# Two-layer decoder trunk on one core: one more pair of rows by seven products in each group of the last stage

## The chip, the cores and the metric

The kernel runs on one core of a Trainium2 chip. Its time is the device time of one execution in microseconds (us). The engines are named as in the profile: PE (TensorE, matmuls; PEld its weight loads), DVE (VectorE), ACT (ScalarE), POOL (GpSimd), SP (SyncE, which issues the loads).

## The reference

Two decoder layers over 256 tokens of width 2048, in float32. Layer 0 mixes tokens by retention, layer 1 by a short convolution; each is followed by a SwiGLU feed-forward network (FFN). Only the last FFN is touched by the change:

```python
D_MODEL, SEQ = 2048, 256
D_FF = 5632

def swiglu(h, w_in, w_out):
    a, b = jnp.split(h @ w_in, 2, axis=-1)
    return (jax.nn.silu(a) * b) @ w_out

h = (rms_norm(x, norm2_g[i]) * (1.0 + sc2) + sh2).astype(x.dtype)
x = (x + g2 * swiglu(h, ffn_w_in[i], ffn_w_out[i])).astype(x.dtype)
...
return rms_norm(x, final_g).astype(x.dtype)
```

## The kernel before

**Precision.** Each weight block and each activation is held as two numbers, `hi` (a cast to the matmul's own float32 form) and `lo` (the rest). A product is three matmuls: hi by hi, hi by lo, lo by hi (`thrice`, L460 to L462). A weight block therefore needs a cast on ACT (L402) and a subtraction on DVE (L405) before PE can use it.

**Loads.** All weights lie in memory in the order of use, in chunks of 128 x 2048 (1 MB). `fetch` issues one chunk on SP into one of three `raw` buffers; it waits until the chunk before in that buffer has been split. `prepare` splits a chunk in pieces; the `hi` and `lo` pieces have four buffers each. `take` hands blocks to PE and prepares up to three pieces (`AHEAD` + 1) beyond the one in use.

**The last stage** is the FFN of layer 1, in two parts of 20 and 24 tiles of 128 hidden columns. The matmuls put tokens on the output's partitions: one covers 128 tokens (of two halves), 128 rows of the weight and 512 of its columns. The last four tiles of part 0 are made first in another form (`first_rows`).

- *First matrix* (`last_input`): ten groups, four in part 0 and six in part 1. A group makes 512 columns of `a` and the matching 512 of `b`, over 16 tiles of rows taken as 8 pairs, 0 to 7. At pair 2 (`TURNS_AT`) of the next group its results are transposed and split for the second matrix (`turned`, L1331 to L1336).
- *Second matrix* (`last_output`): in each part two groups of 1024 output columns, over the part's own rows: 10 pairs in part 0, 12 in part 1. The pairs of part 0 are taken in the order 0, 1, 2, 3, 4, 8, 6, 9, 5, 7. In the last group of part 1 the last three pairs (`TAIL_ROWS`) are the tail: they are taken one column block after the other, and the kernel's end (`added`, `stored`) follows them.

**Pairs in sevens.** A pair of row tiles, two column blocks and two token halves are a 2 x 2 by 2 x 2 product of blocks. Ordinarily it is eight products, 24 matmuls of 128 x 512. A pair of class `Seven` does it with seven products (Winograd's form of Strassen's), 21 matmuls. Which pairs these are is set by `IN_SEVEN` (pairs of each group of the first matrix) and `OUT_SEVEN` (pairs of the second matrix, for part 0 and part 1). For that, three more things are computed:

- *Sums of weights*, in `prepare`: an ordinary chunk is two pieces of 1024 columns (0 and 1). A chunk in sevens is four (2 to 5): a difference of 1024 columns (L391, into the tile `x8` of the page's `x`) and two of 512 (L395, L397) on DVE, and a cast and a `lo` for 1024, 1024, 1024 and 512 columns.
- *Sums of tokens* (`tokens_sums_of`, L1143 to L1146 and two to four splits), once for each pair in sevens: for the first matrix in `made_in_sums` ahead of the ten groups, for the second inside `turned`. They are kept in small tiles (`single_sums`, `tokens_sums`).
- *Sums of products* (`mixed_sums`, L1242 to L1246): after the last seven of a group four banks are combined; in the last group of all they are multiplied by the gate and added (`gated`, L1205, L1206) right there.

PE's order is the order of the program. The instructions of DVE and ACT are put in order by a scheduler.

Of the kernel before, what the change touches and what calls it, by code (L numbers as in the profile page):

```python
# [37 lines left out]
LEAD = 6  # L38
ROOTS_AT, SPREAD_AT = 1, 3
TAIL_ROWS = 6  # L40
IN_SEVEN, OUT_SEVEN, TURNS_AT, BESIDE_CB, BESIDE_SUMS = (3, 4, 6), ((2, 4, 6), (2, 4, 6)), 2, 40, 48
LAST_TILES = 20, 24
STORE_AT, LOAD_AT = 0, 2
LEAD_RET, LEAD_CONV, LEAD_FFN = 6, 4, 2
# [97 lines left out]
class Seven:  # L142
# [6 lines left out]
    n = 2 * DV // P  # L149
# [107 lines left out]
def trunk(ctx: ExitStack, tc: tile.TileContext, x_in, c_in, pos_in, w_mod, cols_in, gain_in, tab_in, w_all, out):  # L257
# [12 lines left out]
    def tmp(tag, shape=(P, S), dtype=F32, pool=work, bufs=None):  # L270
        return pool.tile(list(shape), dtype, tag=tag, name=name(tag), bufs=bufs)
# [90 lines left out]
    in_seven, n = set(), 0  # L362
# [146 lines left out]
    def split(dst, src, at=slice(None)):  # L509

        nc.scalar.copy(dst[:, 0, at], src)
        nc.vector.tensor_tensor(dst[:, 1, at], src, dst[:, 0, at].bitcast(F32), op=ALU.subtract)
# [83 lines left out]
    def scaled_only(layer, norm, j):  # L596

        needed(layer, SC2 if norm else SC1, j)
        a = mod_a[layer][norm][:, j : j + 1]
        high, low = raw_all[:, j, ENDS : ENDS + S], raw_all[:, j, ENDS + S :]  # L600
        nc.scalar.activation(high, x[j], AF.Identity, scale=a)
        nc.vector.scalar_tensor_tensor(low, x[j], a, high.bitcast(F32), op0=ALU.mult, op1=ALU.subtract)
# [50 lines left out]
    def output(groups, act, which, last, after=None, base=None):  # L653

        layer, gate = which[0], mod_g[which[0]][which[1] == GT2]
        first, *groups = groups
        base, acc = first.ks[0] if base is None else base, None
        banks = product(first, act, base, last=False)
        for j, g in enumerate(groups):
            needed(*which, j)  # L660
            col = gate[:, j : j + 1]
            if last and j == KT - 1:
                (pt,) = packed(g, act, base)
                nc.vector.scalar_tensor_tensor(x[j], pt[:, 0, :], col, x[j], op0=ALU.mult, op1=ALU.add)
                acc = [acc, squares(None, x[j], "acc1")]
                if after:
                    after(j)
                return acc
            (pt,) = product(g, act, base, banks=banks[j : j + 1])
            t = tmp("sum", bufs=4)  # L670
            nc.vector.scalar_tensor_tensor(t, pt[:, 1, :], col, x[j], op0=ALU.mult, op1=ALU.add)
            nc.vector.scalar_tensor_tensor(x[j], pt[:, 0, :], col, t, op0=ALU.mult, op1=ALU.add)
            if last:
                acc = squares(acc, x[j])
            if after:
                after(j)


    with ExitStack() as inner:
# [64 lines left out]
        with tc.tile_pool(name="start", bufs=1) as sp:  # L744
# [59 lines left out]
            with tc.manual_schedule(engines={mybir.EngineType.DVE, mybir.EngineType.Activation}):  # L804
# [24 lines left out]
                def square(i):  # L829

                    sq = [rm.tile([P, 2, S], F32, tag=f"mid{2 * i + n}", name=name("sq")) for n in range(2)]
                    for n in range(2):
                        nc.scalar.activation(sq[n], x4[i][:, 2 * n : 2 * n + 2, :], AF.Square)
                    return sq
# [5 lines left out]
                acc = square(0)  # L840
# [197 lines left out]
        def ret_out(part, last):  # L1038
            after = (lambda j: scaled_only(0, 1, j)) if last else None
            acc = output(RET_OUT[part], mid, (0, GT1), last, after, base=0)  # L1040
            assert not asides
            for n in range(len(mid)):
                if ("mid", n) in tag_of:
                    free.append(tag_of.pop(("mid", n)))
            return acc
# [5 lines left out]
        acc = ret_out(1, True)  # L1051
# [16 lines left out]
    for part, groups in enumerate(FFN_IN):  # L1068
# [10 lines left out]
        acc = output(FFN_OUT[part], mid, (0, GT2), part == 1, (lambda j: scaled_only(1, 0, j)) if part else None)  # L1079
# [4 lines left out]
    for i, g in enumerate(CONV_IN):  # L1084
        pending += [sums(g)] if i else normed(acc, 1, 0, g)
        while len(pending) >= 3:
# [3 lines left out]
            b, c, u = pb(tmp("bsum", pool=mpool, bufs=2)), pc(), pu()  # L1090
# [12 lines left out]
    acc = output(CONV_OUT, mid, (1, GT1), True, lambda j: scaled_only(1, 1, j))  # L1103
# [19 lines left out]
    def turn(t, c):  # L1123
# [10 lines left out]
    tokens_sums = [  # L1134
        [v.rearrange("p (i n) -> p i n", i=2)] for v in (in_cb[:, : 6 * P], in_cb[:, 6 * P : 12 * P])
    ] + [[mpool.tile([P, 2, 3 * P], F32R, tag="sums_of_tokens", name="sums_of_tokens")]]
    single_sums = [in_cb[:, n * P : (n + 2) * P].rearrange("p (i n) -> p i n", i=2) for n in (12, 14)]

    def tokens_sums_of(a11, a21, a12, a22, third, others):

        u = tmp("u512", (P, DV), pool=mpool, bufs=3)
        s1, s2, s4, s3 = [u[:, n * P : (n + 1) * P] for n in range(4)]
        nc.vector.tensor_tensor(s3, a11, a21, op=ALU.subtract)  # L1143
        nc.vector.tensor_tensor(s1, a21, a22, op=ALU.add)
        nc.vector.tensor_tensor(s2, s1, a11, op=ALU.subtract)
        nc.vector.tensor_tensor(s4, a12, s2, op=ALU.subtract)  # L1146
        split(third, s3)
        n = 3 * P // len(others)
        for i, dst in enumerate(others):
            split(dst, u[:, i * n : (i + 1) * n])  # L1150

    def parts(both):

        return [both[:, i, t * P : (t + 1) * P] for i in range(2) for t in range(2)]
# [3 lines left out]
    def made_in_sums():  # L1158

        tmp("beside_sums", (P, BESIDE_SUMS), bufs=1)  # L1160
        for tag, n in (("u", 3), ("low", 3), ("sum", 4)):
            single_sums.extend(tmp(tag, (P, 2, P), F32R, bufs=n) for _ in range(n))
        for i in IN_SEVEN:
            both = tmp("u512", (P, 2, S), pool=mpool, bufs=3)
            for n in range(2):
                k = 2 * i + n
                high, low = [h[k].bitcast(F32)[:, v, :] for v in range(2)]
                nc.vector.tensor_tensor(both[:, n, :], high, low, op=ALU.add)
            in_sums[i] = [single_sums.pop() for _ in range(3)]
            tokens_sums_of(*parts(both), h[2 * i][:, :, P:], in_sums[i])  # L1170

    def three(v):
        return [v[0][:, :, n * P : (n + 1) * P] for n in range(3)] if len(v) == 1 else v
# [214 lines left out]
    for part in range(2):  # L1388
        n = LAST_TILES[part] // 2
        mid = mids(LAST_TILES[part]) if part else first_mid  # L1390
        if not part:
            first_rows(mid[-2:])
            made_in_sums()
            ahead_now[0] = AHEAD + 1
        for i, groups in enumerate(LAST_IN[part]):
            due = OUT_SEVEN[part]
            seven = [tokens_sums[due.index(q)] if q in due else None for q in (2 * i, 2 * i + 1)]
            last_input(groups, mid[2 * i : 2 * i + 2], seven)
        act = [mid[k // 2][:, k % 2] for k in range(2 * n)]
        for c, groups in enumerate(LAST_OUT[part]):  # L1400
            last_output(part, 2 * c, groups, act, part * LAST_TILES[0])
# [37 lines left out]
```

## Time and profile before

| | us |
|---|---|
| median of 3 runs | 2595.39 (2594.69 to 2596.74) |
| the profiled execution | 2593.25 |
| its span in the profile | 2591.5 |
| busy of this: PE / PEld / DVE / ACT | 2563.3 / 2236.3 / 2197.4 / 1306.0 |
| one group of the first matrix (1976.7 to 2019.3) | 42.6 |
| a middle group of the second matrix, part 1 (2465.8 to 2530.0) | 64.2 |

The ten groups of the first matrix and the four of the second fill the span from about 1923 us to the end. In rows of the profile a group of instructions is given by line, engine, operation, output and inputs with their shapes, the count, and then busy time and mean duration in ns; behind the second bar stands the engine's idle time before these instructions and what ended it. In a timeline the first column is the start, the second the duration. A row of windows gives each engine's busy time in a stretch of the span, the granted clock of TensorE, and the DMA's share and rate.

### The profile page before, as it was taken

The numbers are of one execution on the slowest core, as the hardware profiler recorded it, in microseconds if no ns is written. First come the engines' busy times: TensorE is split into PE (matmuls) and PEld (weight loads), VectorE is DVE, ScalarE is ACT, GpSimd is POOL, SyncE is SP. The second block draws the span as 40 slices with busy tenths as digits, with TensorE's granted clock in tenths as the row PEclk, the third lists the DMA queues.
The fourth block names the chain that finished last, engine by engine and source line by source line (L and its number), as shares of the span: only waits on it lengthen the run. The fifth ranks groups of instructions, "written<-read, shape, count | busy, mean of one in ns | idle before, by whom it ended". The sixth has DMA issues, their size and how long they took to land.

```text
span 2591.5 us, 36408 instructions
## 1 busy us (share of the span) xinstructions
PE 2563.3 (99%) x14181; PEld 2236.3 (86%) x14181; DVE 2197.4 (85%) x2762; ACT 1306.0 (50%) x1792; POOL 125.9 (5%) x232
## 2 busy tenths in 40 slices
PE   7999999999999999999999999999999999999998
PEld 6898889888889888888888898888998888888887
DVE  7988978787698887777778889988989998999978
ACT  5544543444456545334444454444565554556554
POOL 0000000110000000100001001000000000000001
PEclk9999999999999999999999999999999999999999
DMA  9975768767676888777877768877845565555654
GB/s 398 388 293 209 268 243 306 300 248 277 251 282 246 330 323 307 301 296 298 298 294 283 298 237 313 330 297 277 308 165 210 188 223 205 180 210 187 222 208 147
DMA packets 96688, 689.56 MB, mean 266 GB/s; under 512 B 10737, under 2 KB 12161, under 8 KB 13441
## 3 DMA queue, kind: packets, MB, share of 16 engines
q1 hardware_dynamic: 96514, 687.23, 71.3%
q8 instruction: 111, 1.82, 0.3%
q14 instruction: 63, 0.52, 0.1%
HBM read 685.08 MB, written 2.11 MB: 265 GB/s over the span
## 4 chain that ended last, share of the span: by engine, by line
PE 94%; DVE 3%; DMA 2%; issue 1%; ACT 1%; ACTq 0%; POOLq 0%; POOL 0%; DVEq 0%
PE bank L447 30%; PE bank L450 16%; PE bank L461 12%; PE bank L460 12%; PE bank L462 12%; PE bank L495 2%; PE bank L496 2%; PE bank L494 2%; PE bank L627 1%; PE bank L629 1%; PE bank L628 1%; DVE raw L755 1%; DMA raw<-w_all 1%; DVE lo L405 1%; PE bank L983 1%
## 5 line engine op out<-in xcount | busy, mean ns | idle before, releaser
L402 ACT CAST hi<-raw 128x1024 fp32r<-128x1024 f32 (+1 forms) x954 | 978.9, 1033 | 1015.8 <-PE bank L447 346.4
L405 DVE TENSOR_TENSOR lo<-raw,hi 128x1024 fp32r<-128x1024 f32 (+1 forms) x954 | 1133.9, 1197 | 322.6 <-ACT hi L402 317.3
L447 PE MATMUL bank<-h,hi 128*128 128x512 f32 x2016 | 699.3, 390 | 0.0
L450 PE MATMUL bank<-h,lo 128*128 128x256 f32 x2016 | 568.5, 282 | 0.0
L447 PEld LDWEIGHTS bank<-h,hi 128*128 128x128 f32 x2016 | 378.4, 188 | 79.2
L460 PE MATMUL bank<-hi,h 128*128 128x512 f32 x1032 | 405.0, 392 | 2.2 <-DVE rm L739 2.2
L461 PE MATMUL bank<-lo,h 128*128 128x512 f32 x1032 | 404.3, 392 | 0.0
L462 PE MATMUL bank<-hi,h 128*128 128x512 f32 x1032 | 402.7, 390 | 0.0
L450 PEld LDWEIGHTS bank<-h,lo 128*128 128x128 f32 x2016 | 381.0, 189 | 0.1
L318 DVE SCALAR_TENSOR_TENSOR raw<-raw,cb 128x2048 f32<-128x2048 f32 x160 | 365.5, 2284 | 15.7 <-DMA raw<-w_mod 15.3
L447 PE MATMUL bank<-mid,hi 128*128 128x512 f32 x922 | 319.8, 390 | 0.0
L450 PE MATMUL bank<-mid,lo 128*128 128x256 f32 x922 | 260.1, 282 | 0.4 <-DVE lo L405 0.4
L460 PEld LDWEIGHTS bank<-hi,h 128*128 128x128 f32 x1032 | 194.4, 188 | 40.7 <-DVE rm L739 2.8
L462 PEld LDWEIGHTS bank<-hi,h 128*128 128x128 f32 x1032 | 194.2, 188 | 40.8
L461 PEld LDWEIGHTS bank<-lo,h 128*128 128x128 f32 x1032 | 194.5, 188 | 40.4 <-DVE lo L405 3.3
L447 PEld LDWEIGHTS bank<-mid,hi 128*128 128x128 f32 x922 | 173.1, 188 | 36.2
L450 PEld LDWEIGHTS bank<-mid,lo 128*128 128x128 f32 x922 | 174.2, 189 | 0.7 <-DVE lo L405 0.7
L447 PE MATMUL bank<-rm,hi 128*128 128x512 f32 x496 | 172.5, 390 | 0.0
L496 PE MATMUL bank<-h,lo 128*128 128x256 f32 x512 | 146.4, 286 | 4.6 <-DVE lo L405 4.6
L494 PE MATMUL bank<-h,hi 128*128 128x256 f32 x512 | 146.1, 285 | 3.4 <-ACT h L783 3.4
L495 PE MATMUL bank<-h,hi 128*128 128x256 f32 x512 | 146.1, 285 | 0.7 <-DVE h L784 0.7
L450 PE MATMUL bank<-rm,lo 128*128 128x256 f32 x496 | 139.8, 282 | 0.0
(256 smaller groups left out, 3197.4 us busy)
## 6 DMA issues: line engine op xcount, KB each, us to landing
raw<-w_all SPq DMA_DIRECT2D x456, 1024.0 KB, 4.8
raw<-w_mod SPq DMA_DIRECT2D x192, 1024.0 KB, 5.2
x<-x_in SPq DMA_DIRECT2D x4, 512.0 KB, 5.3
out<-xt SPq DMA_DIRECT2D x4, 512.0 KB, 3.0
decay<-tab_in SPq DMA_DIRECT2D x8, 128.0 KB, 2.4
x<-gate_row SPq DMA_DIRECT2D x2, 512.0 KB, 4.8
last_gain<-gain_in SPq DMA_DIRECT2D x1, 1024.0 KB, 7.2
cols<-cols_in SPq DMA_DIRECT2D x1, 152.0 KB, 8.3
```

Of the source, the lines that this page charges most:

```text
L318: nc.vector.scalar_tensor_tensor(raw, raw, 1.0, cb, op0=ALU.mult, op1=ALU.mult, accum_out=total)
L402: nc.scalar.copy(hi, raw)
L405: nc.vector.tensor_tensor(lo, raw, hi.bitcast(F32), op=ALU.subtract)
L447: nc.tensor.matmul(pt, hi, h, start=fresh and k == g.ks[0], stop=False, skip_group_check=True)
L450: nc.tensor.matmul(pt[:, 1, :], lo, h[:, 0, :], start=False, stop=last and k == g.ks[-1], skip_group_check=True)
L460: nc.tensor.matmul(o, hi, w_hi, start=first, stop=False)
L461: nc.tensor.matmul(o, hi, w_lo, start=False, stop=False)
L462: nc.tensor.matmul(o, lo, w_hi, start=False, stop=last)
L494: nc.tensor.matmul(pt, hi, h[:, 0, :], start=first, stop=False, skip_group_check=True)
L495: nc.tensor.matmul(pt, hi, h[:, 1, :], start=False, stop=False, skip_group_check=True)
L496: nc.tensor.matmul(pt, lo, h[:, 0, :], start=False, stop=last, skip_group_check=True)
L627: nc.tensor.matmul(pt, hi, high, start=k == 0, stop=False, skip_group_check=True)
```

## The change

Pair 5 of every group of the first matrix becomes a pair in sevens, so that pairs 3, 4, 5 and 6 of the eight stand in a row. In the second matrix pair 5 in part 0 and pair 8 in part 1 become pairs in sevens; in the order of use they stand at the places 2, 4, 6 and 8 of ten or twelve. That is 14 pairs in sevens more (56 for 42). The additional sums of tokens get tiles of their own from buffers that are free by then.

```diff
-IN_SEVEN, OUT_SEVEN, TURNS_AT, BESIDE_CB, BESIDE_SUMS = (3, 4, 6), ((2, 4, 6), (2, 4, 6)), 2, 40, 48
+IN_SEVEN, OUT_SEVEN, TURNS_AT, BESIDE_CB, BESIDE_SUMS = (3, 4, 5, 6), ((2, 4, 5, 6), (2, 4, 6, 8)), 2, 40, 48
...
     def made_in_sums():
 
         tmp("beside_sums", (P, BESIDE_SUMS), bufs=1)
-        for tag, n in (("u", 3), ("low", 3), ("sum", 4)):
+        for tag, n in (("acc", 1), ("sq", 2), ("u", 3), ("low", 3), ("sum", 4)):
             single_sums.extend(tmp(tag, (P, 2, P), F32R, bufs=n) for _ in range(n))
         for i in IN_SEVEN:
...
             in_sums[i] = [single_sums.pop() for _ in range(3)]
             tokens_sums_of(*parts(both), h[2 * i][:, :, P:], in_sums[i])
+        tokens_sums.append([single_sums.pop() for _ in range(3)])
```

## The prediction

> **What bounds the kernel now.** I read the page first, then the windows of the last stage, its groups by shape, its waits, and the timelines of VectorE (DVE) and TensorE (PE) in one group of columns. The page gives the whole:
>
> ```profile
> PE 2563.3 (99%) x14181; PEld 2236.3 (86%) x14181; DVE 2197.4 (85%) x2762; ACT 1306.0 (50%) x1792; POOL 125.9 (5%) x232
> PE 94%; DVE 3%; DMA 2%; issue 1%; ACT 1%; ACTq 0%; POOLq 0%; POOL 0%; DVEq 0%
> ```
>
> The chain that ended last is 94% matmul, so over the whole kernel fewer matmuls are less time. The change, though, lies in the last 660 us only, and there the second engine is much fuller than 85%:
>
> ```profile
> core 0: us, PE busy (x) PEld busy (x) DVE busy (x) ACT busy (x) POOL busy (x), PEclk, DMA share, GB/s
> 1976.70:2019.30 42.60, 42.60 (x193) 35.09 (x192) 38.64 (x44) 24.07 (x27) 0.00 (x0) 1.00 0.56 198
> 2061.90:2104.70 42.80, 42.80 (x196) 35.19 (x194) 40.57 (x51) 25.44 (x31) 0.00 (x0) 1.00 0.58 207
> 2338.00:2380.60 42.60, 42.60 (x193) 35.08 (x192) 39.95 (x50) 25.30 (x30) 0.00 (x0) 1.00 0.56 197
> 2530.00:2578.50 48.50, 48.50 (x214) 39.90 (x214) 44.33 (x55) 26.30 (x34) 6.89 (x6) 1.00 0.44 153
> ```
>
> The first three rows are one group each of the first matrix: 8 pairs of rows, three of them in sevens. PE fills them, and DVE has 4.0, 2.2 and 2.65 us to spare. The waits say that this spare time is not DVE's own limit but PE's:
>
> ```profile
> ACT hi L402 <- PE bank L462: 215.6, 224, 1.9
> DVE lo L405 <- ACT hi L402: 58.3, 82, 1.5
> PE bank L461 <- DVE lo L405: 0.5, 1, 0.5
> ```
>
> ScalarE's cast to `hi` waits 224 times for PE to give a weight buffer back, DVE's `lo` waits for that cast, and PE waits for `lo` once in the stage, for 0.5 us. Four buffers of `hi` and `lo` hold the preparation at most three pieces ahead of the matmuls. That lead is the cover on which the change rests.
>
> **What a pair costs on each engine.** On PE, by the starts of matmuls:
>
> ```profile
> 1987.63 0.39 PE L460 MATMUL bank<-hi,low 128*128 128x512 f32 x1
> ...
> 1992.39 0.39 PE L460 MATMUL bank<-hi,h 128*128 128x512 f32 x1
> 1992.71 0.50 PE L461 MATMUL bank<-lo,h 128*128 128x512 f32 x1
> ...
> 2002.82 0.39 PE L460 MATMUL bank<-hi,h 128*128 128x512 f32 x1
> ...
> 2008.26 0.39 PE L460 MATMUL bank<-hi,h 128*128 128x512 f32 x1
> ```
>
> 1987.63 to 1992.39 is a pair in sevens, 21 matmuls in 4.76 us; 2002.82 to 2008.26 is an ordinary one, 24 in 5.44 us. So one matmul costs 0.227 us (0.39 is its pipelined length), and a seven saves 0.68 us of PE. On DVE:
>
> ```profile
> L405 DVE TENSOR_TENSOR lo<-raw,hi 128x1024 fp32r<-128x1024 f32 x251 | 303.6, 1220 | 53.5 <-ACT hi L402 50.5
> L391 DVE TENSOR_TENSOR x<-raw 128x1024 f32<-128x1024 f32 x42 | 51.1, 1217 | 0.3 <-DMA raw<-w_all 0.3
> L397 DVE TENSOR_TENSOR raw<-raw 128x512 f32<-128x512 f32 x42 | 29.0, 690 | 1.0
> L405 DVE TENSOR_TENSOR lo<-raw,hi 128x512 fp32r<-128x512 f32 x42 | 28.8, 686 | 6.7 <-ACT hi L402 6.5
> L395 DVE TENSOR_TENSOR raw<-raw,x 128x512 f32<-128x512 f32 x42 | 28.7, 683 | 0.0
> ```
>
> These are 42 pairs in sevens. Each takes four instructions of 1024 columns (L391, `lo` three times) and three of 512 (L395, L397, `lo`). Neighbours overlap by some 0.08 us, as the starts in the next timeline show (1990.30 to 1991.43; 2003.26 to 2003.86), so I price them at 1.14 and 0.60: 4 x 1.14 + 3 x 0.60 = 6.36 us. An ordinary pair is two `lo`: 2.28 us. A pair turned into sevens thus gives PE 0.68 us and gives DVE 4.08 us, and a pair in sevens takes DVE 6.36 us where PE takes 4.76: within a run of sevens DVE is the slower engine by 1.60 us a pair, and the lead is spent.
>
> **First matrix, ten groups (pair 5 becomes a seven).** By the sum alone a group would still nearly fit: 2.65 us spare against 4.08 added and 0.68 less time. What decides is that pairs 3, 4, 5, 6 now stand in a row. Here is DVE in the group that began at 1976.5, pair 5 still ordinary:
>
> ```profile
> 1988.56 1.82 DVE L405 TENSOR_TENSOR lo<-raw,hi 128x1024 fp32r<-128x1024 f32 x2
> 1990.30 1.22 DVE L391 TENSOR_TENSOR x<-raw 128x1024 f32<-128x1024 f32 x1
> 1991.43 3.49 DVE L405 TENSOR_TENSOR lo<-raw,hi 128x1024 fp32r<-128x1024 f32 x3
> 1994.84 1.22 DVE L405 TENSOR_TENSOR lo<-x,hi 128x1024 fp32r<-128x1024 f32 x1
> ...
> 1997.85 1.83 DVE L405 TENSOR_TENSOR lo<-raw,hi 128x1024 fp32r<-128x1024 f32 x2 [0.47 <-ACT hi L402]
> 2000.74 2.60 DVE L405 TENSOR_TENSOR lo<-raw,hi 128x1024 fp32r<-128x1024 f32 x2 [1.07 <-ACT hi L402]
> 2003.26 0.68 DVE L1243 TENSOR_TENSOR u<-bank,x 128x512 f32<-128x512 f32 x1
> 2003.86 1.22 DVE L405 TENSOR_TENSOR lo<-raw,hi 128x1024 fp32r<-128x1024 f32 x1
> ```
>
> At 1990.30 DVE has finished the weights of pair 4 (the second `lo` of the first row is its last block) while PE is still in it until 1992.39: a lead of 2.1 us. Nothing before this point changes in the group, so I go on from here with the order of DVE's instructions in the changed program: L391, `lo`, L395, `lo`, L397, `lo`, `lo` for pair 5, and the same for pair 6. Pair 5 ends at 1990.30 + 6.36 = 1996.66. In pair 6 the third `lo` starts after two of 1024, L391 and one more of each kind, 1996.66 + 3 x 1.14 + 2 x 0.60 = 2001.28, and has landed 1.22 later, at 2002.50. PE then has five matmuls left with that piece and three with the last block: 8 x 0.227 = 1.82. A matmul that restarts after a wait costs about 0.1 more (1992.39 to 1992.71 above is 0.32, not 0.227). Pair 6 ends at 2004.42. It ended at 2002.82, so the group is **1.6 us longer**, where PE alone would have made it 0.68 shorter. The last block's `lo` (landed by 2003.1) is not late. Afterwards the lead comes back: until the next sevens PE has four ordinary pairs (21.8 us) against four times 2.28 and twelve DVE instructions of 512 that fold the results (7.2), 16.3 us. So the cost neither grows nor is made up; ten groups make +16.0. Bounds: +1.4 a group if the price is 1.13 and the restart free, and +2.1 if one of the two pairs shows one wait for the cast of 0.47 us, as in the row of 1997.85.
>
> **New sums of tokens.** One set more is built ahead of the stage, one in each part while a group is turned (L1143 to L1146, then splits):
>
> ```profile
> L1143 DVE TENSOR_TENSOR u<-u 128x128 f32<-128x128 f32 x9 | 2.5, 283 | 0.0
> L1168 DVE TENSOR_TENSOR u<-h 128x256 f32<-128x256 f32 x6 | 2.4, 418 | 0.0
> L512 DVE TENSOR_TENSOR in_cb<-u,in_cb 128x384 fp32r<-128x384 f32 x4 | 2.2, 550 | 0.0
> ```
>
> Five instructions of 0.28 and one of 0.55, less the overlap of 0.08 each, are 1.5 us on DVE. In part 0 pairs 4 and 5 of the second matrix come from one group, so two sets are built just before the same four sevens, in the group of 2061.90 with 2.2 us to spare: I put all 1.5 on the path (0 to 2.0). In part 1 the extra set falls in a group that had none; groups with one and with none both take 42.6 us, so nothing (0 to 1.5). The set ahead of the stage has two L1168 besides, 2.2 us, with PE in long ordinary work: +1.0, between 0 and 2.2.
>
> **Second matrix, four groups.** The sevens stand at every second place, with an ordinary pair between (PE 4.76 + 5.44 = 10.20, DVE 6.36 + 2.28 = 8.64), so the gain is real: three groups x -0.68 = -2.0. The fourth is the end of the kernel. Its last seven was pair 6, with pairs 7 and 8 behind it; now it is pair 8, with the tail behind it. Four sums (L1243 to L1246) and eight gated additions follow the last seven, 12 x 0.60 = 7.2 us of DVE. They now meet the tail's six `lo` (6.84) and the first column's six instructions of 512 (3.6): 17.6 us against the tail's 72 matmuls, 16.3 us. In the trace of before DVE waits 0.56, 1.49 and 0.59 us there:
>
> ```profile
> 2570.08 1.23 DVE L405 TENSOR_TENSOR lo<-raw,hi 128x1024 fp32r<-128x1024 f32 x1 [0.56 <-ACT hi L402]
> 2572.80 1.23 DVE L405 TENSOR_TENSOR lo<-raw,hi 128x1024 fp32r<-128x1024 f32 x1 [1.49 <-ACT hi L402]
> ```
>
> So I expect PE to wait 17.6 - 16.3 + 0.1 = 1.4 us for a `lo` behind these twelve. The first column's two products with the gain, which now fit into that idle time, come so late that they stand before the second column's additions, which close the kernel: 2 x 0.60 = 1.2. That is +2.6 (0 to 7.2, all twelve uncovered), less 0.68: +1.9. Loads are unchanged in number and size.
>
> **Sum.** 16.0 + 1.5 + 1.0 - 2.0 + 1.9 = +18.4 us. The profiled execution took 2593.25 us (span 2591.5 and 1.75 around it), which becomes 2611.7; the median of the runs, 2595.39, is 2.1 above it, and becomes 2613.8. With all terms low (14.0 + 0 + 0 - 2.0 - 0.7) it is +11, with all high (21 + 2.0 + 1.5 + 2.2 - 2.0 + 6.5) +31.
>
> **Rivals.** (1) *PE stays the bound, faster.* If DVE kept up everywhere, 14 sevens x 0.68 = 9.5 us go: 2585.9. For it: PE 99%, DVE spare in every window, and waits that are PE's. It decides at the third `lo` of pair 6: it must land by about 2000.3, when PE at full pace (pair 6 ending at 2002.14) asks for it; I have 2002.50, so DVE would need 2.2 us more lead, and the four buffers forbid it. Chance 0.04. The Trainium skill has a rule that bears on this: Perfetto Trace Analysis, section Identifying the Most-Contended Engine, says to optimize first the engine with the highest occupancy, taking busy LDWEIGHTS for TensorE. By the page's shares (86 against 85%) that would still be TensorE, and the change would win its 9.5 us; by the windows (35.08 of 42.6 is 82%, against DVE's 39.95, 94%) it is VectorE, to which the change adds. The same section speaks of regimes whose most-contended engine changes over time; I go by the window. (2) *No change.* The idle time in front of pairs 3 and 4 is used for a deeper lead than I allow, the groups cost about nothing (0 instead of 1.6), and the rest nets +2.4: 2597.8. Chance 0.05. (3) *Hand-offs show in a run of sevens.* A block passes DVE, then ScalarE, then DVE again; where L395 or L397 stands right before the `lo` that needs it, DVE waits for the cast. At 0.47 in each of three pairs of ten groups it is 14 us more: +32, 2627.8. Against it: the built order puts another `lo` between nearly everywhere. Chance 0.12. The forecast has 0.79.
>
> **Numbers.** A measurement of this kernel can tell about 0.2% (5.2 us) from no change. The range goes from 2606 (all terms low) to 2625 (near all high); rivals 1, 2 and most of 3 are left out. Faster 0.04, same 0.05, slower 0.91.
>
> **What would show it.** In the changed profile the waits of PE for `lo` (L405) grow from 0.5 us in one to 20 to 30 us in many, each under a microsecond but at the third and fourth seven of a group; the windows of a group go from 42.6 to about 44.2, with DVE over 42 us busy; DVE's waits for `hi` fall below half of 58.3; the groups of the second matrix, but for the last, lose 0.7. Groups of 41.9 us without waits of PE prove me wrong towards rival 1, and waits of DVE for ScalarE inside the sevens towards rival 3.

## The result and the profile after

The changed kernel takes 2611.79 us (median of 4 runs, 2609.26 to 2612.3) against 2595.04 us of the kernel before on the same chip (median of 4): a ratio of 1.0063, interval 1.0045 to 1.008, that is 12 to 21 us more. The spans of the two profiled executions, 2609.9 and 2591.5 us, differ by 18.4 us.

The page after, busy time and the chain that ended last:

```profile
PE 2566.8 (98%) x14139; PEld 2224.7 (85%) x14139; DVE 2253.7 (86%) x2858; ACT 1327.9 (51%) x1834; POOL 140.4 (5%) x232
PE 85%; DVE 11%; DMA 1%; issue 1%; ACT 1%; POOL 0%; ACTq 0%; POOLq 0%; DVEq 0%
```

42 matmuls fewer by the program's count, and yet TensorE's share of the chain falls from 94 to 85% while VectorE's rises from 3 to 11%. The busy rows alone (98%, 86%) hardly show it; the chain does. The rows below are windows of four groups of the first matrix. Each begins with the transposes of one group's results, which stand at pair 2 of the group behind it, and ends with the transposes of the next:

```profile
core 0: us, PE busy (x) PEld busy (x) DVE busy (x) ACT busy (x) POOL busy (x), PEclk, DMA share, GB/s
1978.67:2022.95 44.28, 43.43 (x190) 34.16 (x189) 42.28 (x50) 25.65 (x29) 0.00 (x0) 1.00 0.51 190
2022.95:2067.19 44.24, 43.39 (x189) 34.15 (x188) 43.67 (x56) 26.86 (x32) 0.00 (x0) 1.00 0.51 191
2067.19:2113.57 46.38, 42.94 (x191) 34.41 (x190) 45.27 (x62) 27.26 (x36) 0.00 (x0) 1.00 0.54 199
2349.89:2394.13 44.24, 43.40 (x190) 34.16 (x189) 43.67 (x56) 26.85 (x32) 0.00 (x0) 1.00 0.51 190
```

A group takes 44.24 us where it took 42.6, VectorE is busy in 43.67 of them where the group has a set of token sums to build (42.28 where it has none, first row, with the same time), and the weight loads, which the change makes fewer, fall to 34.16. The granted clock stays at 1.00. The waits of the last stage:

```profile
ACT hi L402 <- PE bank L462: 171.0, 161, 3.0
PEld bank L461 <- DVE lo L405: 36.5, 58, 1.7
DVE lo L405 <- ACT hi L402: 20.3, 32, 1.5
PE bank L461 <- DVE lo L405: 9.7, 14, 1.3
```

Before the change TensorE's wait for `lo` was 0.5 us, once, in the matmuls' rows, and in those of its weight loads:

```profile
PEld bank L461 <- DVE lo L405: 4.6, 12, 1.0
```

Now it is 9.7 us in the matmuls' rows and 36.5 in those of their weight loads; the two overlap, so they are not added. The prediction had named 20 to 30 us in many waits as its sign. The matmuls' rows alone fall short of that; by the starts of the matmuls from 1931 us on, the spacings that are over 0.15 us too long add up to 21.2 us (51 of them), against 0.7 (one) before. VectorE's wait for the cast falls from 58.3 to 20.3 us: its spare time is used up.

Where the 18.4 us lie, by the same marks in both traces (transposes; after less before): ahead of the stage +0.09; the first group with what is built ahead of it +2.05; the next two groups +1.67 and +1.63; the group with two sets of token sums 46.38 - 42.72 = +3.66; the second matrix of part 0 with the first group of part 1, 147.78 - 148.18 = -0.40; five groups of part 1, +1.63 to +1.69 each, +8.26; the second matrix of part 1 and the end, 127.27 - 125.83 = +1.44. That sums to 18.4. The rows of the three terms that are not a plain group, before, and then the second of them after (after, the first stands above and the third below, with the run on the last group):

```profile
2061.75:2104.47 42.72, 42.72 (x193) 35.11 (x192) 40.49 (x51) 25.44 (x31) 0.00 (x0) 1.00 0.59 208
2104.47:2252.65 148.18, 147.64 (x654) 121.73 (x653) 130.32 (x151) 77.43 (x84) 0.00 (x0) 1.00 0.57 203
2465.67:2591.50 125.83, 116.89 (x519) 96.33 (x517) 100.65 (x119) 62.42 (x77) 8.02 (x8) 0.98 0.50 176
...
2113.57:2261.35 147.78, 146.91 (x646) 119.78 (x645) 141.58 (x168) 82.30 (x92) 0.00 (x0) 1.00 0.56 201
```

VectorE in the group that the prediction walked through (its transposes begin at 1978.67, those of before at 1976.53):

```profile
1990.70 1.82 DVE L405 TENSOR_TENSOR lo<-raw,hi 128x1024 fp32r<-128x1024 f32 x2
1992.44 1.22 DVE L391 TENSOR_TENSOR x<-raw 128x1024 f32<-128x1024 f32 x1
...
1998.78 1.23 DVE L391 TENSOR_TENSOR x<-raw 128x1024 f32<-128x1024 f32 x1
...
2003.39 4.16 DVE L405 TENSOR_TENSOR lo<-raw,hi 128x1024 fp32r<-128x1024 f32 x4
```

and TensorE at the end of its pair 6:

```profile
2004.20 0.40 PE L460 MATMUL bank<-hi,h 128*128 128x512 f32 x1
2004.67 0.50 PE L461 MATMUL bank<-lo,h 128*128 128x512 f32 x1
2005.01 0.39 PE L462 MATMUL bank<-hi,h 128*128 128x512 f32 x1
...
2006.62 0.39 PE L460 MATMUL bank<-hi,h 128*128 128x512 f32 x1
```

From the transposes to the L391 after pair 4 it is 13.77 us, as before (1990.30 - 1976.53). From there VectorE has no gap: the next L391 comes 6.34 us later, and the third `lo` of pair 6 starts 4.61 after that, at 2003.39. TensorE's L461 at 2004.67 follows on its landing (2003.39 + 1.22 = 2004.61), and pair 7 begins at 2006.62: 27.95 us after the transposes, where it was 26.29. That is 1.66 us for the group.

### The profile page after: what moved, and what is told of

Read it like the earlier page. It is cut to its first block, busy times and chain, and to the rows that moved or that the text cites. A ratio compares the mean times of both kernels' runs of the same rounds, so it can differ in the third digit from the quotient of the medians.

```text
span 2609.9 us, 36477 instructions
## 1 busy us (share of the span) xinstructions
PE 2566.8 (98%) x14139; PEld 2224.7 (85%) x14139; DVE 2253.7 (86%) x2858; ACT 1327.9 (51%) x1834; POOL 140.4 (5%) x232
## 3 DMA queue, kind: packets, MB, share of 16 engines
HBM read 685.08 MB, written 2.11 MB: 263 GB/s over the span
## 4 chain that ended last, share of the span: by engine, by line
PE 85%; DVE 11%; DMA 1%; issue 1%; ACT 1%; POOL 0%; ACTq 0%; POOLq 0%; DVEq 0%
PE bank L447 29%; PE bank L450 16%; PE bank L461 10%; PE bank L462 9%; PE bank L460 9%; DVE lo L405 6%; PE bank L496 2%; PE bank L495 2%; PE bank L494 2%; PE bank L627 1%; PE bank L629 1%; PE bank L628 1%; DVE x L391 1%; DVE raw L755 1%; DMA raw<-w_all 1%
## 5 line engine op out<-in xcount | busy, mean ns | idle before, releaser
L405 DVE TENSOR_TENSOR lo<-raw,hi 128x1024 fp32r<-128x1024 f32 (+1 forms) x968 | 1140.9, 1192 | 276.0 <-ACT hi L402 268.6
L461 PE MATMUL bank<-lo,h 128*128 128x512 f32 x992 | 390.0, 393 | 4.9 <-DVE lo L405 3.4
L460 PE MATMUL bank<-hi,h 128*128 128x512 f32 x992 | 389.6, 393 | 1.2 <-DVE rm L739 1.2
L462 PE MATMUL bank<-hi,h 128*128 128x512 f32 x992 | 387.1, 390 | 0.0
L461 PEld LDWEIGHTS bank<-lo,h 128*128 128x128 f32 x992 | 186.9, 188 | 48.9 <-DVE lo L405 13.6
L462 PEld LDWEIGHTS bank<-hi,h 128*128 128x128 f32 x992 | 186.6, 188 | 39.0
L460 PEld LDWEIGHTS bank<-hi,h 128*128 128x128 f32 x992 | 186.8, 188 | 38.7 <-DVE rm L739 1.8
```

The lines of the kernel that those rows point to most:

```text
L405: nc.vector.tensor_tensor(lo, raw, hi.bitcast(F32), op=ALU.subtract)
L460: nc.tensor.matmul(o, hi, w_hi, start=first, stop=False)
L461: nc.tensor.matmul(o, hi, w_lo, start=False, stop=False)
L462: nc.tensor.matmul(o, lo, w_hi, start=False, stop=last)
```

## The experiments

My theory: within a row of four sevens VectorE's own time is the pace, and it costs 1.6 us in each of ten groups; the rest of the change is small and of both signs. The rivals: every added pair costs, wherever it stands; the hand-off between VectorE and ScalarE sets the pace; VectorE's sum over a whole group decides, not the row. Every edit below is made to the changed kernel; every time stands against the kernel before, run beside it on the same chip.

**Only the second matrix**

```diff
-IN_SEVEN, OUT_SEVEN, ... = (3, 4, 5, 6), ((2, 4, 5, 6), (2, 4, 6, 8)), ...
+IN_SEVEN, OUT_SEVEN, ... = (3, 4, 6), ((2, 4, 5, 6), (2, 4, 6, 8)), ...
```

> Only the second matrix has the added pairs (first matrix 3, 4, 6 as before). My theory (VectorE is too slow in the run of four sevens, and the rest is small): three groups x -0.68, the last group +1.9, the group that builds two sets of token sums 0 to +1.5: between -1 and +2 us against before. If it were the number of added pairs in sevens that costs, wherever they stand (18.4 us for 14), four of them would cost +5. If TensorE set the pace everywhere: -2.7.

2592.43 us against 2593.64, ratio 0.9998 (0.9989 to 1.0007): no difference. Its windows, from the group with two sets of token sums, over part 0's second matrix, to the end:

```profile
2061.25:2105.08 43.83, 43.37 (x194) 34.96 (x192) 41.93 (x57) 26.20 (x34) 0.00 (x0) 1.00 0.55 202
2105.08:2250.85 145.77, 145.77 (x648) 120.76 (x647) 137.87 (x163) 80.96 (x90) 0.00 (x0) 1.00 0.57 206
2463.74:2591.00 127.26, 115.62 (x513) 95.23 (x511) 108.45 (x129) 65.45 (x81) 9.32 (x8) 0.97 0.48 174
```

Against 42.72, 148.18 and 125.83 of before: +1.1, -2.4, +1.4. Gain and losses cancel. A fixed cost for each added pair (+5 for these four) is ruled out: the interval is -3 to +2 us. That TensorE sets the pace everywhere (-2.7) lies within it, and falls with the next run.

**Only the first matrix**

```diff
-IN_SEVEN, OUT_SEVEN, ... = (3, 4, 5, 6), ((2, 4, 5, 6), (2, 4, 6, 8)), ...
+IN_SEVEN, OUT_SEVEN, ... = (3, 4, 5, 6), ((2, 4, 6), (2, 4, 6)), ...
```

> Only the first matrix has the added pair (second matrix 2, 4, 6 as before). My theory: ten groups x +1.6 and +1 ahead of the stage: +16 to +18 against before, groups of 44.2 us. Cost by number of added pairs: +13. TensorE bound: -6.8.

2608.74 against 2593.64 us, ratio 1.0064 (1.0049 to 1.0079): the interval is +13 to +20 us, all of the loss, with groups of 44.24 to 44.42. TensorE as the pace (-6.8) is ruled out; cost by number (+13) lies at the edge of the interval and fell with the run before.

**Two subtractions left out in pair 5 of the first matrix**

```diff
+        elif piece == 4 and chunk in light:
+            pass
         elif piece == 4:
             nc.vector.tensor_tensor(b[1], b[2], differences[:, :DV], op=ALU.subtract)
         elif piece == 5:
-            nc.vector.tensor_tensor(b[3], b[3], b[1], op=ALU.subtract)
+            if chunk not in light:
+                nc.vector.tensor_tensor(b[3], b[3], b[1], op=ALU.subtract)
             raw = b[3]
```

`light` holds the chunks of pair 5 of the first matrix.

> As the changed kernel, but in pair 5 of the first matrix the two subtractions of 512 columns (L395, L397) are left out, so that pair computes with other weights: VectorE has 1.2 us less in each row of four, everything else stays. My theory: VectorE's own time is the pace in the row, so each group loses those 1.2 us: 43.0 instead of 44.2, 12 us less than the changed kernel, +6 against before. Rival (ScalarE's casts or the hand-off between the engines set the pace): less than 4 us of change.

2600.17 against 2593.64 us, ratio 1.0034 (1.0021 to 1.0047). Groups fall from 44.24 to 43.18 us:

```profile
2298.02:2341.20 43.18, 42.84 (x190) 34.30 (x189) 42.56 (x54) 26.54 (x32) 0.00 (x0) 1.00 0.52 196
```

1.2 us of VectorE's work in the row is worth 1.06 us of the group. By itself this run does not part VectorE's own time from the hand-off to ScalarE, because two casts of pair 5 no longer wait for a subtraction. The trace of the changed kernel does: through pairs 5 and 6 of the group shown above ScalarE waits 0.69 to 1.33 us for VectorE ahead of each cast that needs a difference, while VectorE goes on without a gap. So VectorE sets the pace there, and ScalarE does not.

**The same left out in all four pairs**

> The changed kernel, with L395 and L397 left out in all four pairs in sevens of each group of the first matrix (those pairs compute with other weights). VectorE has 5.16 us for such a pair, TensorE 4.77, and 4.8 us less in a group. My theory: TensorE is the pace again, groups of 41.9 us, that is 0.7 less than before: -5 to -8 against before. Rival (casts or hand-offs set the pace in a row of sevens): groups over 43.

2586.25 against 2593.26 us, ratio 0.9974 (0.9963 to 0.9985), with the added pairs of the second matrix in it. A group:

```profile
2289.69:2331.63 41.94, 41.94 (x190) 34.47 (x188) 38.96 (x46) 26.77 (x32) 0.00 (x0) 1.00 0.54 200
```

TensorE is busy throughout again, and the group is 0.65 us shorter than before: about what three matmuls take. In such a group the change then pays what its count of matmuls says.

**No row of four: pairs 2, 3, 5, 6**

```diff
-IN_SEVEN, OUT_SEVEN, ... = (3, 4, 5, 6), ((2, 4, 5, 6), (2, 4, 6, 8)), ...
+IN_SEVEN, OUT_SEVEN, ... = (2, 3, 5, 6), ((2, 4, 5, 6), (2, 4, 6, 8)), ...
```

> As the changed kernel, but pairs 2, 3, 5, 6 of the first matrix are in sevens, with the ordinary pair 4 between: the same instructions in number, none in a row of four. My theory (the row of four uses up the lead): the ordinary pair gives 3.16 us of lead back, the waits of TensorE for lo nearly vanish and the groups fall to 41.9 to 42.6: -8 to +2 against before, 16 to 26 less than the changed kernel. Rival (the sum of VectorE's work in a group is what is too much, however it is ordered): groups stay at 44.2, +16 to +18.

2611.9 against 2593.64 us, ratio 1.0077 (1.006 to 1.0094). My expectation was wrong; the total is the rival's, no better than the row of four. A group without a set of token sums, then one with, then another without:

```profile
1979.39:2021.59 42.20, 42.14 (x190) 34.41 (x189) 41.88 (x49) 25.64 (x29) 0.00 (x0) 1.00 0.54 199
2304.64:2349.69 45.05, 42.57 (x189) 34.46 (x188) 44.65 (x56) 26.64 (x32) 0.00 (x0) 1.00 0.50 187
...
2259.78:2304.64 44.86, 43.27 (x189) 34.22 (x188) 43.46 (x51) 26.41 (x30) 0.00 (x0) 1.00 0.51 187
```

The first falls to 42.20 as my theory says; the second is full on VectorE (44.65 of 45.05). Its instructions, 4 x 6.36 + 4 x 2.28 + 7.2 + 1.5 = 43.3 us, are more than TensorE's 41.9, whatever their order. So there is a second limit close to the first, VectorE's sum over a group.

The sum alone does not give this order's time, though. From 2304.64 to 2483.08 four groups with a set take 44.6 us each, VectorE being busy for 43.8 of them, and the third row has no set and takes 44.86. Two things differ here besides the row. Pair 2 is now a seven, so the split of the transposed results and the sums of tokens (L1337, L1143 to L1146) fall into the first run of two, and behind them, in the second row, TensorE's matmuls of 2310.30 and 2314.60 are followed by waits of 1.2 and 1.6 us. And this trace has two stretches of 3.4 us at a granted clock of 0.50, in which matmuls start 0.43 us apart in place of 0.227; they cost at most some 3 us of the 18. How much of the time each of these makes was not tried.

The next two runs leave the same work out of both orders.

**Work of VectorE left out outside the row.** Without the four additions that fold a group's ordinary pairs into its sevens:

```diff
         ours, extra = gathered(groups, h, 0, in_sums)
-        for (t, j), pt in ours.items():
-            nc.vector.tensor_tensor(extra[t, j], pt, extra[t, j], op=ALU.add)
```

> The changed kernel without the four additions (L1318) that fold a group's ordinary pairs into its sevens at the end of a group (the result lacks the ordinary pairs). VectorE has 2.4 us less in a group, all of it outside the row of four. If the row decides (my prediction): groups stay at 44.2, within 2 us of the changed kernel in all. If VectorE's sum over the group decides (43.7 busy of 44.2): groups fall to 42 to 42.5, about 18 us less than the changed kernel.

> The same four additions left out, with the pairs 2, 3, 5, 6 in sevens. With the additions this order was no better than the row of four. If the sum was what held it (43.3 us of VectorE in a group with a set of token sums, 40.9 without the additions), groups now fall to 41.9 to 42.6: within 4 us of before, 14 or more below the row of four without the additions. If the order of sevens doesn't matter: the same time as that run.

With the row of four 2611.52 us, ratio 1.0071 (1.0056 to 1.0086); with two and two 2596.35 us, ratio 1.0012 (1.0002 to 1.0021). A group of each, the row of four first:

```profile
2305.54:2349.77 44.23, 43.40 (x189) 34.16 (x188) 41.53 (x51) 26.76 (x32) 0.00 (x0) 1.00 0.52 189
...
2293.93:2336.49 42.56, 42.31 (x189) 34.47 (x188) 41.98 (x51) 26.45 (x32) 0.00 (x0) 1.00 0.53 198
```

In the row of four 2.4 us less on VectorE change nothing: 44.23 for 44.24, now with 2.7 us idle that do not help, because they lie ahead of pair 5 or behind the row: from 2315.79, within pair 4, to behind the row VectorE still has no gap. With two and two the same 2.4 us bring a group from 44.6 to 42.56. Once the sum fits, the order alone makes 1.67 us a group, 15 us in all. In the changed kernel the row decides; behind it, 0.6 us lower by VectorE's busy time (43.67 of 44.24) and 0.9 by the price (43.3), lies the sum.

**The last group with three sevens**

```diff
-        out.append(in_pairs(cols, rows[: len(rows) - rest], OUT_SEVEN[part]))
+        out.append(in_pairs(cols, rows[: len(rows) - rest], OUT_SEVEN[part][: 3 if rest else 4]))
...
-        sums = {i: three(v) for i, v in zip(OUT_SEVEN[part], tokens_sums)}
+        sums = {i: three(v) for i, v in zip(OUT_SEVEN[part], tokens_sums[: 3 if final else 4])}
```

Its pair 8 is multiplied with a sum of tokens in place of the second half of the activations; the amount of work is that of an ordinary pair.

> The changed kernel, but the very last group (second matrix, part 1, output columns 1024 to 2047) keeps its three pairs 2, 4, 6 in sevens. By the prediction the added pair cost +1.9 there (a wait of 1.4 and 1.2 at the end, less 0.68): 2 us less than the changed kernel, +14 to +17 against before, the wait of TensorE near the end gone. If the late sums were hidden after all: 0.7 more than the changed kernel.

2609.99 against 2592.54 us, ratio 1.0061 (1.0043 to 1.0078): in the total not to be told from the changed kernel's 1.0063. The window from the last transposes to the end tells it, the changed kernel first:

```profile
2482.63:2609.90 127.27, 115.61 (x513) 95.23 (x511) 109.09 (x130) 65.45 (x81) 16.79 (x8) 0.97 0.48 174
...
2480.62:2605.70 125.08, 116.21 (x516) 95.77 (x514) 105.44 (x125) 63.99 (x79) 8.03 (x8) 0.97 0.47 177
```

2.2 us less, as forecast: the wait of TensorE's weight loads for `lo` in this stretch goes from 1.7 to 0.3 us, and from the start of the last matmul to the end it takes 9.29 us in place of 10.73. The added pair costs more at the end of the kernel than it saves.

**The subtractions on GpSimd**

```diff
-            nc.vector.tensor_tensor(b[1], b[2], differences[:, :DV], op=ALU.subtract)
+            nc.gpsimd.tensor_tensor(b[1], b[2], differences[:, :DV], op=ALU.subtract)
         elif piece == 5:
-            nc.vector.tensor_tensor(b[3], b[3], b[1], op=ALU.subtract)
+            nc.gpsimd.tensor_tensor(b[3], b[3], b[1], op=ALU.subtract)
```

> The changed kernel with the two subtractions of 512 columns of every pair in sevens (L395, L397) on GpSimd in place of VectorE; nothing left out. VectorE then has 5.16 us for a pair in sevens where TensorE has 4.77, and 4.8 us less in a group: 43.7 busy becomes 38.9 of 41.9. My theory (VectorE's time is the pace): the row of four now falls behind by 1.6 us at most, which the lead covers; groups of 41.9 to 42.3 us, -4 to -8 against before, 20 to 24 less than the changed kernel. Rival (the order of the pieces or ScalarE's casts set the pace): groups stay over 43.5. If a subtraction on GpSimd takes far over 1.2 us or holds VectorE up, the casts of the third and fourth piece come late: slower than before.

> Both together: subtractions of the sevens on GpSimd, and three pairs in sevens in the last group. My theory: thirteen added pairs x -0.68 = -8.8, the group with two sets of token sums perhaps 1 us late: -6 to -9 us against before, faster than both kernels. If GpSimd holds VectorE up: no gain.

2656.9 us, ratio 1.0242 (1.0224 to 1.026), and 2655.29 us, ratio 1.0243 (1.0224 to 1.0262): the slowest of all. Both forecasts missed; what came is the last sentence of each. The first run's groups by shape, its timeline and a group:

```profile
L395 POOL TENSOR_TENSOR raw<-raw,x 128x512 f32<-128x512 f32 x56 | 133.1, 2377 | 408.8 <-DVE x L391 264.6 <-ACT hi L402 144.2
L405 DVE TENSOR_TENSOR lo<-x,hi 128x1024 fp32r<-128x1024 f32 x56 | 90.9, 1623 | 12.9 <-ACT hi L402 12.2
```

```profile
2335.89 1.30 POOL L397 TENSOR_TENSOR raw<-raw 128x512 f32<-128x512 f32 x1
2336.17 2.11 DVE L405 TENSOR_TENSOR lo<-x,hi 128x1024 fp32r<-128x1024 f32 x1 [1.49 <-ACT hi L402]
```

```profile
2334.85:2382.45 47.60, 43.94 (x190) 33.99 (x189) 45.83 (x46) 26.55 (x32) 17.48 (x9) 1.00 0.46 177
```

A subtraction of 0.69 us on VectorE is 2.38 on GpSimd, and VectorE's own `lo` beside it is stretched from 1.22 us to 1.62 in the mean. With ten instructions fewer in a group VectorE is busy for 45.83 us where it was 43.67: the move gave it more time to spend, not less. So this says nothing against the theory; it failed as a relief. None of these runs is a version with the full work that is faster than both kernels.

## Why the prediction was right, point by point

*VectorE, not TensorE, paces a run of sevens.* Shown: the timeline has no gap on VectorE from pair 5 to pair 6, taking its work away there shortens the group (1.06 for 1.2 us), taking 2.4 us away elsewhere does not (44.23), and taking enough away gives TensorE's own time (41.94). The price of 6.36 us a pair was 6.34.

*+1.6 us a group.* Measured 1.63 to 1.69 in the seven groups that have a window of their own, so ten groups make some 16.5 for 16.0.

*Token sums.* The group with two sets costs 3.66, of which 1.65 is the row: 2.0 for the 1.5 forecast, at its upper bound. Without the row the same two sets cost 1.1 (only the second matrix). The set ahead of the stage was put at 1.0 and is, by difference, 2.05 - 1.65 = 0.4. The extra set in part 1 costs nothing, as forecast, but with little to spare: VectorE is busy for 43.79 of that group's 44.25 us.

*Second matrix.* Three groups at -0.68 were right in kind; part 0 gives -0.40 - 1.65 = -2.05 rather than -1.36, because a wait of TensorE at 2110.14 in the trace of before, 0.69 beyond the usual spacing, is gone. I had left it out. (The -1.65 is an assumption for the first group of part 1; the run with the second matrix alone, where that group has no row of four, shows -2.41 in this window.) Part 1 was put at -0.68 + 1.9 = +1.2 and is +1.44. The wait in the tail is there, at the place forecast:

```profile
2592.66 0.50 PE L461 MATMUL bank<-lo,mid 128*128 128x512 f32 x1 [1.29 <-DVE lo L405]
```

The matmul before it began at 2590.98, so it is 1.45 us beyond the usual spacing, for 1.4; after the last matmul the end comes 1.4 us later, for 1.2.

*What I had wrong without its showing in the sum.* "By the sum alone a group would still nearly fit" is wrong by the prediction's own figures: 2.65 us of spare time less 0.68 is 1.97, against 4.08 added, so 2.1 us too much; and the window with 2.65 has a set of token sums in it already. By the price, six groups of ten do not fit by their sum (43.3 against 41.9), and breaking up the row did not save them. "The lead comes back" held in this order: groups with a set and without one take the same 44.24 to 44.30 us. But it left the 1.5 us of token sums out of its 16.3, and it took for spare what another order of the pairs would have needed. The row decides, as forecast, yet its 44.2 lies only 0.6 to 0.9 us above a limit that I had dismissed: that the total did not suffer from this is in part luck. The small terms were off by up to 0.7 us each, of both signs, and cancel.

*Shares of the span and of the window.* The Trainium skill, Perfetto Trace Analysis, section Identifying the Most-Contended Engine, gives the answer of the wrong sign by the shares of the whole span (86% weight loads against 85% VectorE), and the right one by those of the window (94% VectorE against 82% weight loads). The runs decide for the window. What the prediction says of regimes stands in that page's next section, Optimization Strategy.

## What to carry to other kernels

Price a trade of matmuls for vector work in the stage where it lands, as a rate: here 0.68 us of TensorE for 4.08 of VectorE, 6.36 against 4.76 us while the run of such work lasts, with a lead of three pieces at most from four buffers. Then check two limits separately, the run (does the lead last) and the whole period (does the sum fit); idle time that lies outside the run pays for nothing inside it. Where the last piece of such work feeds the end of a kernel, count what then stands behind it: here it cost 2.2 us more than in the group without it.

## What the runs showed of the hardware that I had not expected

GpSimd beside VectorE is far from free: a 128 x 512 subtraction took 2.38 and 1.97 us in the mean (L395, L397), 1.30 in the timeline above, and VectorE's two-input instructions beside it were held up: the `lo` that starts 0.28 us after GpSimd's subtraction takes 2.11 us, which is the other's remaining 1.02 and about its own 1.22. The waiting goes both ways. Of 96 instructions of VectorE that begin inside a GpSimd subtraction and take over 1.3 us, all but one end a fixed time after it, 0.55 us with 512 columns and 1.08 to 1.09 with 1024. Of the 112 subtractions on GpSimd the 12 that begin with no VectorE instruction under way take 1.3 us; most of the others take 2.1 to 2.3, so much of the mean of 2.38 is waiting. (GpSimd's spans in a profile are rough.) The Trainium skill (SBUF — State Buffer, section SBUF: two separate sides) states a lock of just this kind: a GpSimd instruction that reads SBUF and a VectorE instruction with two inputs from SBUF share a pair of ports, and the one that starts first holds it for its whole length. The trace agrees with that row: 24 of the 56 `lo` of that form (L405, `lo<-x,hi`) take 2.1 us or more, the other 32 take 1.2.

After a matmul that had to wait, the next one starts 0.34 us later instead of 0.227 (2004.67 to 2005.01), after a long wait as after a short one. These short waits leave the granted clock alone: the four windows after, in which TensorE is idle for 0.8 to 3.4 us, show 1.00. The one window of a group in these runs with less is that of the group with two sets of token sums in the run with pairs 2, 3, 5, 6:

```profile
2066.64:2112.73 46.09, 43.92 (x190) 35.64 (x189) 45.41 (x61) 28.20 (x36) 0.00 (x0) 0.96 0.55 205
```

Within it the clock is 0.50 for 3.4 us from 2073.9 on, and matmuls start 0.43 us apart; the stretch begins 0.6 us after the end of a single wait of 2.2 us. The same run has another such stretch from 1940.8 on, 1.1 us after a wait of 1.6. That such waits lower the clock isn't shown: in the run with the subtractions on GpSimd TensorE has a wait of 2.5 us in this stage, and the clock stays at 1.00.
